# Sums of squares spread over the places of the first stage, a later first attention group, and four buffers of cosines and sines

## The chip, the cores and the metric

The kernel runs on one core of one Trainium2 chip. The metric is the device time of one execution in microseconds (us), as the median of several runs; a profiled execution gives the trace. The engines are named as in the profile: PE (TensorE, matmuls), PEld (its weight loads), DVE (VectorE), ACT (ScalarE), POOL (GpSimd) and SP (SyncE, which only issues DMAs here).

## The reference

One inference step of a hybrid encoder layer, on 2048 prompt frames and 64 frames of a running stream, 2112 tokens of width 1024 in all, in float32:

```
xn = rmsnorm(x, norm_mix)                      # x * rsqrt(mean(x*x) + eps) * g
proj = xn @ w_in                               # 1024 x 5632: x_rnn, y_gate, q, k, v, g_rnn, g_attn
xc = causal_dwconv(x_rnn); h = rg_lru(xc)      # width-4 conv, gated linear recurrence
y_rnn = h * gelu(y_gate)
q, k = rope_partial(q), rope_partial(k)        # first 16 dims of each head of 64
y_attn = band_attention(q, k, v, sinks)        # 16 heads, 4 KV heads, chunks of 64, window 128
mixed = sigmoid(g_rnn) * y_rnn + sigmoid(g_attn) * y_attn
x = x + mixed @ w_out
x = x + ConvFFN(rmsnorm(x, norm_ffn))          # up 5632, width-3 conv, silu(gate) * val, down
y = rmsnorm(x, norm_final)
```

The outputs are y and the new key, value, recurrence and convolution states.

## The kernel before

Tokens stand in the free dimension and features in the 128 partitions. A float32 matmul is done as three matmuls of rounded parts: each operand is split into a high part (a copy that rounds, on ACT, line 204) and a low part (the rest, on DVE, line 205), and `mm3` (lines 237 to 239) multiplies high by high, low by high and high by low. A tile of 128 output features of one block of tokens takes 8 k-tiles, so 24 matmuls.

The first stage, which the change touches, runs in three sets of two blocks: 320, 320, then 384, 384, then 352, 352 tokens (`SETS`). For each set the 44 column tiles of `w_in` pass by. `kept` brings a tile's weights: in the first set the raw weights are loaded (line 226, tiles `wraw`, which lie in a region of SBUF called FW), split into `whl` (three buffers), and the split form is stored to DRAM (`wiS`, on POOL's queue); in the later sets the split form is loaded from there (line 223). PSUM has three banks (`pmm`, name "mm") for the results of projections.

A set begins with q, k and v. Two tiles hold the rotated parts of q: `trig` loads a block's cosines and sines (tiles named "h", lines 395 and 396), `rope` (lines 375 to 381) multiplies the two PSUM results by them, and `qparts` splits and stores the result to DRAM (`qS`, line 390). The same follows for k, then v and the other q tiles.

Then come four groups `g`, one for each KV head. `key_prep` reads the keys and values back and splits them (kA, kB, vv). `rnn` is a generator that computes two channel tiles of the recurrent branch: 18 steps, here called places, numbered j = 0 to 17. A channel's places are two of x (with the convolution), two of y, one of the gates (lines 652 to 656) with the scan after it, two of g and two of a; most hold one projection of 24 matmuls. `attention` is a second generator, advanced once at each place: a unit of 128 queries has its scores S and softmax at one place (lines 547 to 565), its transposes (line 572) three places later, and its products Y (lines 580, 581) a place after that; in between the next unit's queries are loaded from `qS` (line 539: D twice, E once). The products of a group with the gates (`mix`) are put off to the next group's place 3.

The next set's tokens are prepared in groups 2 and 3. `stats` loads x (line 255, tiles `xk`), squares each k-tile on ACT (lines 257 and 259) and adds the squares on POOL (line 260), 16 k-tiles in a set; its `finish` makes the reciprocal root (lines 263 to 266), called at place 6 of group 3. Then `apply` scales and splits the tokens. In the kernel before, all of `stats` is written at place 8 of group 2.

What sets the order: in the first stage a scheduler that works with its own estimates of durations sorts each engine's instructions, so an instruction can stand some places ahead of where it is written; each engine then runs its list strictly in order, and SP and POOL also issue their DMAs in order. `with behind()` puts the DMAs of its block behind the last weight load on their queue. The second stage (output projection and feed-forward part) is scheduled by hand and is not touched.

Of the kernel before, what the change touches and what calls it, by code (L numbers as in the profile page):

```python
# [7 lines left out]
F32 = mybir.dt.float32  # L8
F32R = mybir.dt.float32r
AF = mybir.ActivationFunctionType  # L10
ALU = mybir.AluOpType
# [3 lines left out]
P = 128  # L15
T = 2112
TP = 2048
KO = 8
# [3 lines left out]
SETS = [[(0, 320), (320, 320)], [(640, 384), (1024, 384)], [(1408, 352), (1760, 352)]]  # L22
BN = 384
# [103 lines left out]
def kernel(ctx: ExitStack, tc: tile.TileContext, xT, w_in, w_out, w_up, w_dn, gw, pk,  # L127
                             sinks, cq, sq, ck, sk, kcT, vcT, kcn, vcn, augk, auge, ident_in,
                             yT, kpT, ksT, vpT, vsT, kc_o, vc_o, h_o, lc_o, fc_o):
    nc = tc.nc  # L130
# [21 lines left out]
    FW = Region(tc, "FW", 23712, F32)  # L152
    fw = Pool(FW)
# [61 lines left out]
    def behind():  # L215
        return tc.issue_after(lastw[0].ins)
# [30 lines left out]
        xblocks[t0] = (pool.tile([P, KO, BN], F32R, name="xh", bufs=2), pool.tile([P, KO, BN], F32R, name="xl", bufs=2))  # L247
        return xblocks[t0]

    def stats(t0, n):  # L250
        r = fw.tile([P, BN], F32, name="nr", bufs=2)[:, :n]
        s = fw.tile([P, BN], F32, name="ns", bufs=2)[:, :n]
        for k in range(KO):
            x = fw.tile([P, BN], F32, name="xk", bufs=4)[:, :n]
            nc.sync.dma_start(x, xT[k * P:(k + 1) * P, t0:t0 + n])
            if k == 0:
                nc.scalar.activation(s, x, AF.Square)
            else:
                nc.scalar.activation(x, x, AF.Square)
                nc.gpsimd.tensor_tensor(s, s, x, op=ALU.add)  # L260

        def finish():
            p = pmm.tile([P, 512], F32, name="mm")
            nc.tensor.matmul(p[:, :n], ones, s, start=True, stop=True)
            nc.scalar.activation(r, p[:, :n], AF.Sqrt, scale=1.0 / 1024, bias=epst)
            nc.vector.reciprocal(r, r)
            rstd[t0] = r
        return finish

    def apply(blocks):  # L270

# [38 lines left out]
    with tc.tile_pool(name="sp", bufs=1) as sp:  # L310
# [9 lines left out]
        for i, (t0, n) in enumerate(SETS[0]):  # L320
# [9 lines left out]
            r = sp.tile([P, BN], F32, name="nr", bufs=2)[:, :n]  # L330
# [3 lines left out]
            for k in range(KO):  # L334
                x = xt[:, k, :n]
# [3 lines left out]
        consts()  # L339

    es1 = ExitStack()

    FX = Region(tc, "FX", 4096, F32, "right")
    es1.callback(FX.close)
    fw.regions = (FW, FX)
    fw.extend("wraw", KO * P, 1)
    ap = es1.enter_context(tc.tile_pool(name="ap", bufs=1, reuse_waits="tile", side="right"))
    rp_ = es1.enter_context(tc.tile_pool(name="rp", bufs=2, reuse_waits="tile", side="right"))
    pat = es1.enter_context(tc.tile_pool(name="pat", bufs=1, space=PSUM))
# [40 lines left out]
            nc.sync.dma_start(qS[i, r0:r0 + 128, tt], t[:, :n].bitcast(F32))  # L390

    def trig(c, s, r, tt, n):
        ct = rp_.tile([P, BN], F32, name="h")
        st = rp_.tile([P, BN], F32, name="h")
        nc.sync.dma_start(ct[:r, :n], c[:, tt])
        nc.sync.dma_start(st[:r, :n], s[:, tt])
        return ct, st
# [53 lines left out]
    for si, blocks in enumerate(SETS):  # L451
# [5 lines left out]
        for t0, n in blocks:  # L457
            tt = slice(t0, t0 + n)
            ct, st = trig(cq, sq, P, tt, n)
            a, b = rope(proj(wa, t0, n), proj(wb, t0, n), P, ct, st, n)  # L460
            qparts(a[:, :n], 0, tt, n)
            qparts(b[:, :n], 128, tt, n)
# [3 lines left out]
        for t0, n in blocks:  # L466
            tt = slice(t0, t0 + n)
            ct, st = trig(ck, sk, 32, tt, n)
# [121 lines left out]
        def attention(g, kv):  # L590
            units = [attn_s(g, u, kv) for u in qts]
            next(units[0])
            for i, u in enumerate(units):
                next(u)
                if i:
                    next(units[i - 1])
                yield
                if i:
                    next(units[i - 1])
                yield  # L600
                if i + 1 < len(units):
                    next(units[i + 1])
                yield
            next(units[-1])
            yield
            next(units[-1])
            yield
# [116 lines left out]
        def rnn(g, rr, ta):  # L724
            for i in range(2):
                c, st = 2 * g + i, {}
                yield from rnn_x(c, st)
                yield from rnn_y(c, st)
                for bi in range(len(blocks)):
                    rnn_gates(c, st, bi)  # L730
                yield
                rnn_scan(c, st)
                yield from rnn_g(c, st, rr[i])
                yield from rnn_a(c, ta[i])

        nxt = []
        for g in range(4):
            kv = key_prep(g)
            ya = ap.tile([P, 2, SN], F32, name="ya")
            rr = [rp_.tile([P, SN], F32, name=f"rr{i}", bufs=1) for i in range(2)]  # L740
            ta = [[], []]
            at = attention(g, kv)
            for j, _ in enumerate(rnn(g, rr, ta)):
                next(at, None)
                if j == 3:
                    while pending:
                        pending.pop(0)()
                if g == 2 and j == 8 and si + 1 < len(SETS):
                    with behind():
                        nxt = [stats(t0, n) for t0, n in SETS[si + 1]]  # L750
                if g == 3 and j == 6:
                    for f in nxt:
                        f()
                if g == 3 and nxt:

                    if j == (16 if si == 0 else 8):
                        ahead = apply(SETS[si + 1])
                    if j in ((16, 17) if si == 0 else (9, 13, 15)):
                        with behind():
                            next(ahead)  # L760
            if g == 3 and nxt:
                for _ in ahead:
                    pass
            if g == 1 and si == 2:

                fw.close()
                xk, raws = Pool(FW), Pool(FW, right=True)
                xk.reserve("xk", BS, 16)
                raws.reserve("wraw", 4 * P, 2)
                mixed = mixes(0, xk)  # L770
                with behind():
                    next(mixed)
                    wload(0)
                    wload(1)
            if g == 3 and si == 2:

                es0.close()
                RA = Region(tc, "RA", 58368, F32R)
                mixp, wh0 = [Pool(RA), None, None], Pool(RA)
                wh0.reserve("wh", 8 * P, 4)  # L780
            for _ in at:
                if g == 3 and si == 2:
                    next(mixed)
                    next(mixed)
                    next(mixed)
            for i in range(2):
                pending.append(lambda i=i, rr=rr, ta=ta, ya=ya, g=g, blocks=blocks, s0=s0:
                               mix(2 * g + i, rr[i], ta[i], ya[:, i], blocks, s0))
# [539 lines left out]
    dmade, dloaded, dweights, draws_, toks, fetched, raw = [0] * 7, [0] * 7, {}, {}, {}, [0], {}  # L1328
# [67 lines left out]
    for i in range(3):  # L1396
# [7 lines left out]
        if i == 0:  # L1404
            xk = Pool(FW)
# [5 lines left out]
        for m in range(8):  # L1411
# [17 lines left out]
            if i == 0 and m == 5:  # L1429
                drive(side, 99)  # L1430
                xk.close()
                xk = Pool(FW, right=True)
# [49 lines left out]
    for i, (lanes, fresh, u) in enumerate(plan):  # L1482
# [61 lines left out]
        if i in (11, 18):  # L1544
            t0, n = PAIRS[2][i == 18]
# [117 lines left out]
    for j, (i, p, k, ms, cs) in enumerate(seq):  # L1663
# [54 lines left out]
        for m in ms:  # L1718
            r = {q: R[p, q][:, m, cs] for q in ("11", "12", "21", "22")}
# [152 lines left out]
```

## Time and profile before

| what | value |
| --- | --- |
| median of 3 runs | 2969.44 us (2962.66 to 2976.83) |
| profiled execution: its own time | 2964.2 us |
| profiled execution: span of the trace | 2962.4 us |
| mean granted PE clock | 0.983 |
| busy: PE, DVE, ACT, POOL | 96%, 69%, 51%, 14% |

The span runs from the first to the last instruction on the core. In rows of the timeline the first number is the start in us, the second the duration; brackets give how long the engine had been idle before and what released it. "SPq" is SP's queue of DMA issues; its duration there is that of issuing, not of the transfer. In rows of waits the numbers are the total in us, how often, and the longest. In windows the numbers behind the window's length are the busy us of PE, PEld, DVE, ACT and POOL with their instruction counts, then the PE clock granted, the DMA engines' share and GB/s.

### The profile page before, as it was taken

To read this page: it belongs to the slowest core of one execution; us is meant where nothing else is said; L and a number is where in the kernel's file an instruction comes from. 1 tells how busy PE (TensorE), PEld (TensorE's weight loads), DVE (VectorE), ACT (ScalarE), POOL (GpSimd) and SP (SyncE) were. 2 spreads that over 40 slices of the span, in tenths; PEclk is the share of its full clock that TensorE was granted. 3 is DMA by queue.
4 is the path that set the end of the run, shared out by engine and by line. 5 is a ranking of instruction groups with operands and counts; after the bars stand their busy time and mean duration, and the time that the engine had idled before them with its cause. 6 is when DMAs were issued, how large, how long until landed. Compare 5 with 4: busy or idle time off the path is not lost.

```text
span 2962.4 us, 48650 instructions
## 1 busy us (share of the span) xinstructions
PE 2856.2 (96%) x17572; PEld 2749.1 (93%) x17572; DVE 2037.4 (69%) x3998; ACT 1507.7 (51%) x3353; POOL 400.6 (14%) x699
## 2 busy tenths in 40 slices
PE   7999899999999999998898999999899999999998
PEld 6899899999999999998898999999799999999997
DVE  6388784467686277776567988888756557656686
ACT  4377772466654266665324555555544444333442
POOL 2012100000200000002321323333111111000011
PEclk8999999999999999999999999999999999999999
DMA  7867656644455745436875656565766666977573
GB/s 250 282 210 229 193 198 226 193 149 135 152 162 169 244 141 182 147 125 247 274 234 178 219 195 220 200 221 201 259 202 219 215 223 210 278 208 223 162 231 112
DMA packets 337042, 601.13 MB, mean 203 GB/s; under 512 B 39216, under 2 KB 236832, under 8 KB 319904
## 3 DMA queue, kind: packets, MB, share of 16 engines
q1 hardware_dynamic: 288096, 409.28, 44.9%
q0 software_dynamic: 48704, 188.73, 16.8%
q8 instruction: 139, 2.28, 0.3%
q14 instruction: 103, 0.84, 0.1%
HBM read 398.11 MB, written 200.29 MB: 202 GB/s over the span
## 4 chain that ended last, share of the span: by engine, by line
PE 61%; issue 15%; DVE 10%; DMA 8%; ACT 3%; POOL 2%; SPq 0%; POOLq 0%; DVEq 0%; ACTq 0%
PE mm L237 9%; PE mm L239 9%; PE mm L238 9%; PE mf L1157 3%; PE mf L1159 3%; PE mf L1158 3%; PE mf L1678 2%; PE mf L1677 2%; PE mf L1679 2%; DMA x1S<-FW 2%; PE mm L1159 2%; PE mm L1157 2%; PE mm L1158 2%; PE pt L572 2%; DMA FW<-in_xT_dram 1%
## 5 line engine op out<-in xcount | busy, mean ns | idle before, releaser
L237 PE MATMUL mm<-xh,whl 128*128 128x320 f32 (+2 forms) x2112 | 691.1, 327 | 12.6 <-DVE y L379 9.6
L238 PE MATMUL mm<-xl,whl 128*128 128x320 f32 (+2 forms) x2112 | 687.2, 325 | 5.4 <-DVE xl L205 4.7
L239 PE MATMUL mm<-xh,whl 128*128 128x320 f32 (+2 forms) x2112 | 685.9, 325 | 0.0
L209 ACT ACTIVATE RE<-FW 128x512 fp32r<-128x512 f32 (+2 forms) x540 | 288.0, 559 | 398.9 <-DVE FW L1036 98.2
L210 DVE TENSOR_TENSOR RE<-FW,RE 128x512 fp32r<-128x512 f32 (+2 forms) x540 | 313.4, 602 | 161.1 <-ACT RE L209 156.1
L237 PEld LDWEIGHTS mm<-xh,whl 128*128 128x128 f32 x2112 | 401.7, 190 | 19.7 <-DVE y L379 11.1
L238 PEld LDWEIGHTS mm<-xl,whl 128*128 128x128 f32 x2112 | 401.8, 190 | 12.2 <-DVE xl L205 8.0
L239 PEld LDWEIGHTS mm<-xh,whl 128*128 128x128 f32 x2112 | 401.4, 190 | 0.8
L1193 DVE SCALAR_TENSOR_TENSOR FA<-FA,pkt 128x608 f32<-128x608 f32 (+1 forms) x264 | 245.4, 950 | 51.1 <-ACT FA L1187 46.5
L1157 PE MATMUL mf<-RA,RE 128*128 128x304 f32 (+1 forms) x604 | 198.9, 329 | 12.5 <-ACT FW L1202 5.5
L1159 PE MATMUL mf<-RA,RE 128*128 128x304 f32 (+1 forms) x604 | 198.1, 328 | 0.0
L1158 PE MATMUL mf<-RA,RE 128*128 128x304 f32 (+1 forms) x604 | 197.5, 327 | 0.0
L1677 PE MATMUL mf<-RE 128*128 128x304 f32 (+1 forms) x594 | 192.9, 325 | 1.8 <-DVE RR L1722 1.8
L1678 PE MATMUL mf<-RE 128*128 128x304 f32 (+1 forms) x594 | 192.7, 324 | 0.6 <-DVE RE L210 0.5
L1679 PE MATMUL mf<-RE 128*128 128x304 f32 (+1 forms) x594 | 191.2, 322 | 0.0
L1158 PE MATMUL mf<-RE 128*128 128x304 f32 (+1 forms) x484 | 158.3, 327 | 4.1 <-DVE RE L210 4.1
L550 DVE TENSOR_REDUCE mx<-S 128x4 f32<-128x1024 f32 (+1 forms) x68 | 81.0, 1191 | 117.9 <-PE S L548 117.9
L1157 PE MATMUL mf<-RE 128*128 128x304 f32 (+1 forms) x484 | 158.3, 327 | 3.1 <-ACT RE L209 3.1
L1187 ACT ACTIVATE FA<-FA,pkt 128x608 f32<-128x608 f32 (+1 forms) x132 | 128.1, 970 | 64.0 <-DVE FA L1208 59.5
L1159 PE MATMUL mf<-RE 128*128 128x304 f32 (+1 forms) x484 | 158.2, 327 | 0.0
L559 ACT ACTIVATE pr<-S,nm 128x256 f32<-128x256 f32 (+1 forms) x272 | 124.0, 467 | 27.9 <-DVE nm L553 27.3
L1157 PEld LDWEIGHTS mf<-RA,RE 128*128 128x128 f32 x604 | 114.8, 190 | 17.8 <-ACT FW L1202 6.1
(335 smaller groups left out, 6954.7 us busy)
## 6 DMA issues: line engine op xcount, KB each, us to landing
whl<-wiS SPq DMA_DIRECT2D x88, 1024.0 KB, 5.3
wiS<-whl POOLq DMA_DIRECT2D x44, 1024.0 KB, 6.9
wuS<-RE POOLq DMA_DIRECT2D x88, 512.0 KB, 4.0
RE<-wuS SPq DMA_DIRECT2D x88, 512.0 KB, 4.4
FW<-in_w_up_dram SPq DMA_DIRECT2D x154, 256.0 KB, 4.1
hS<-FA POOLq DMA_DIRECT2D x154, 152.0 KB, 3.8
FW<-hS SPq DMA_DIRECT2D x154, 152.0 KB, 3.8
FW<-in_w_in_dram SPq DMA_DIRECT2D x44, 512.0 KB, 5.3
```

The costliest lines, as they stand in the source:

```text
L209: lastact[0] = nc.scalar.activation(hi, src, AF.Copy)
L210: return lambda: nc.vector.tensor_tensor(lo, src, hi.bitcast(F32), op=ALU.subtract)
L237: nc.tensor.matmul(ps[:, :n], wh[:, c], xh[:, k, :n], start=first, stop=False)
L238: nc.tensor.matmul(ps[:, :n], wh[:, c], xl[:, k, :n], start=False, stop=False)
L239: nc.tensor.matmul(ps[:, :n], wl[:, c], xh[:, k, :n], start=False, stop=last)
L1157: nc.tensor.matmul(ps[:, :n], w[:, 0, c], x[:, k, 0], start=first, stop=False, **more)
L1158: nc.tensor.matmul(ps[:, :n], w[:, 0, c], x[:, k, 1], start=False, stop=False, **more)
L1159: nc.tensor.matmul(ps[:, :n], w[:, 1, c], x[:, k, 0], start=False, stop=last, **more)
L1193: nc.vector.scalar_tensor_tensor(uc, G[:, j:j + self.cols], col("fw", 44 * j + m), uc, op0=ALU.mult, op1=ALU.add)
L1677: nc.tensor.matmul(ps[m][:, cs], w[:, 0, c], t[:, 0], start=k == 0, stop=False)
L1678: nc.tensor.matmul(ps[m][:, cs], w[:, 0, c], t[:, 1], start=False, stop=False)
L1679: nc.tensor.matmul(ps[m][:, cs], w[:, 1, c], t[:, 0], start=False, stop=k == 10)
```

## The change

It has four parts. `stats` becomes a generator over both blocks of a set: the first step loads two k-tiles, and each further step squares one k-tile, adds it and loads the one two ahead; it is advanced once at each place from place 4 of group 2 to place 4 of group 3. In the very first group the attention is not advanced at places 0 and 1, and twice at places 7 and 13. The tiles "h" get four buffers instead of two. The region FX (4096 bytes in each partition), through which the raw weights had a third buffer, goes: two raw weight buffers are left in the first set. For `apply`, the `xk` tiles have nine buffers in both kernels.

```
-    def stats(t0, n):
-        r = fw.tile([P, BN], F32, name="nr", bufs=2)[:, :n]
-        s = fw.tile([P, BN], F32, name="ns", bufs=2)[:, :n]
-        for k in range(KO):
-            x = fw.tile([P, BN], F32, name="xk", bufs=4)[:, :n]
-            nc.sync.dma_start(x, xT[k * P:(k + 1) * P, t0:t0 + n])
-            if k == 0:
-                nc.scalar.activation(s, x, AF.Square)
-            else:
-                nc.scalar.activation(x, x, AF.Square)
-                nc.gpsimd.tensor_tensor(s, s, x, op=ALU.add)
-        def finish():
...
+    def stats(blocks, done):
+        todo = [(t0, n, k) for t0, n in blocks for k in range(KO)]
+        raw = []
+        def load(j):
+            if j < len(todo):
+                t0, n, k = todo[j]
+                raw.append(fw.tile([P, BN], F32, name="xk", bufs=4)[:, :n])
+                nc.sync.dma_start(raw[j], xT[k * P:(k + 1) * P, t0:t0 + n])
+        def finish(t0, n, r, s):
...
+        load(0)
+        load(1)
+        yield
+        for j, (t0, n, k) in enumerate(todo):
+            x = raw[j]
+            if k == 0:
+                r = fw.tile([P, BN], F32, name="nr", bufs=2)[:, :n]
+                s = fw.tile([P, BN], F32, name="ns", bufs=2)[:, :n]
+                nc.scalar.activation(s, x, AF.Square)
+                done.append(lambda t0=t0, n=n, r=r, s=s: finish(t0, n, r, s))
+            else:
+                nc.scalar.activation(x, x, AF.Square)
+                nc.gpsimd.tensor_tensor(s, s, x, op=ALU.add)
+            load(j + 2)
+            yield
...
-    FX = Region(tc, "FX", 4096, F32, "right")
-    es1.callback(FX.close)
-    fw.regions = (FW, FX)
-    fw.extend("wraw", KO * P, 1)
...
-        ct = rp_.tile([P, BN], F32, name="h")
-        st = rp_.tile([P, BN], F32, name="h")
+        ct = rp_.tile([P, BN], F32, name="h", bufs=4)
+        st = rp_.tile([P, BN], F32, name="h", bufs=4)
...
             for j, _ in enumerate(rnn(g, rr, ta)):
-                next(at, None)
+                if (si, g) != (0, 0) or j > 1:
+                    next(at, None)
+                if (si, g) == (0, 0) and j in (7, 13):
+                    next(at, None)
...
-                if g == 2 and j == 8 and si + 1 < len(SETS):
+                if g == 2 and j == 4 and si + 1 < len(SETS):
+                    squares_ = stats(SETS[si + 1], nxt)
+                if si + 1 < len(SETS) and (g == 2 and j > 3 or g == 3 and j < 5):
                     with behind():
-                        nxt = [stats(t0, n) for t0, n in SETS[si + 1]]
+                        next(squares_, None)
```

Line numbers in the order of the changed kernel are higher by 9 to 15 behind `stats` (rope's stores are line 399, the loads of cosines and sines 404 and 405).

SP's queue at the start of set 1, in the kernel before (`h` are cosines and sines, `whl` weights, `qS` the stores of q):

```order
L223 DMA whl<-wiS 128x2048
L390 DMA qS<-xch 128x384
L390 DMA qS<-xcl 128x384
L395 DMA h<-in_cq_dram 128x384
L396 DMA h<-in_sq_dram 128x384
L223 DMA whl<-wiS 128x2048
L395 DMA h<-in_ck_dram 32x384
```

The same place in the changed kernel:

```order
L223 DMA whl<-wiS 128x2048
L399 DMA qS<-xch 128x384
L399 DMA qS<-xcl 128x384
L404 DMA h<-in_ck_dram 32x384
L405 DMA h<-in_sk_dram 32x384
L404 DMA h<-in_ck_dram 32x384
```

The second block's pair for q, 128x384, has gone from here; it now stands with the first block's pair in set 0, behind the first stores of k. The second weight load of the rows before now follows the second block's stores.

ACT at the beginning of the first group's places, before (`xc`, `xr`, `xch` belong to the x places, `pr` and `es` to the softmax of the first unit, `y` to the y places):

```order
L623 ACTIVATE xc<-mm,pkt 128x320
L628 ACTIVATE xr<-mm 128x320
L204 ACTIVATE xch<-xc 128x320
L559 ACT_TABLE_LOAD
L559 ACTIVATE pr,sm<-S,nm 128x128 x4
L561 ACTIVATE es<-es 128x4
L623 ACTIVATE xc<-mm,pkt 128x320
L628 ACTIVATE xr<-mm 128x320
L204 ACTIVATE whl<-FW 128x1024
L688 ACTIVATE y<-mm 128x320
```

The same in the changed kernel:

```order
L632 ACTIVATE xc<-mm,pkt 128x320
L637 ACTIVATE xr<-mm 128x320
L204 ACTIVATE whl<-FW 128x1024
L697 ACTIVATE y<-mm 128x320
L204 ACTIVATE xch<-xc 128x320
L679 ACT_TABLE_LOAD
L679 ACTIVATE y<-y 128x320
L568 ACT_TABLE_LOAD
L568 ACTIVATE pr,sm<-S,nm 128x128 x4
L570 ACTIVATE es<-es 128x4
L697 ACTIVATE y<-mm 128x320
```

The first softmax has moved behind both x places and the first y, and has a table load before it. On PE the first unit's scores stand 48 matmuls later than before.

ACT in group 2 of set 0, before, around the first y place (`FW` and `FX` in lines 257 and 259 are the squares):

```order
L204 ACTIVATE xch<-xc 128x320
L559 ACTIVATE pr,sm<-S,nm 128x128 x4
L561 ACTIVATE es<-es 128x4
L259 ACTIVATE FX<-FX 128x384
L623 ACTIVATE xc<-mm,pkt 128x320
L628 ACTIVATE xr<-mm 128x320
L204 ACTIVATE whl<-FW 128x1024
L259 ACTIVATE FW<-FW 128x384 x2
L688 ACTIVATE y<-mm 128x320
```

The same in the changed kernel (line 279 is the square):

```order
L204 ACTIVATE xch<-xc 128x320
L568 ACTIVATE pr,sm<-S,nm 128x128 x4
L570 ACTIVATE es<-es 128x4
L632 ACTIVATE xc<-mm,pkt 128x320
L637 ACTIVATE xr<-mm 128x320
L204 ACTIVATE whl<-FW 128x1024
L279 ACTIVATE FW<-FW 128x384 x2
L697 ACTIVATE y<-mm 128x320
```

Before, these two squares are the 13th and 14th of the 16 and two more follow before the second y; in the changed kernel they are the 7th and 8th, and the next pair stands at the next scan.

More of the change, by code (lines that the diff above doesn't have):

```diff
@@ L267, in finish @@
             rstd[t0] = r
-        return finish
+        load(0)
[13 more added lines that the diff above has]
+            yield
     def apply(blocks):
```

## The prediction

> **What bounds the kernel now.** I read the page, then TensorE's waits over the whole run, then the busy time and granted clock in short windows around the longest waits.
>
> ```profile
> span 2962.4 us, 48650 instructions
> ...
> PE 2856.2 (96%) x17572; PEld 2749.1 (93%) x17572; DVE 2037.4 (69%) x3998; ACT 1507.7 (51%) x3353; POOL 400.6 (14%) x699
> ```
>
> TensorE (PE) is busy 96% of the span, and its work stays as it is. Time can only come from places where PE stands still or runs at a lowered clock. Its waits (in total, times, longest):
>
> ```profile
> PE mm L237 <- DVE y L379: 9.6, 5, 3.6
> PE mm L652 <- ACT y L688: 5.8, 2, 3.6
> PE S L547 <- DMA D<-qS: 5.2, 1, 5.2
> PE Y L581 <- DVE pl L205: 4.5, 6, 2.3
> PE mm L237 <- ACT ta L475: 1.2, 1, 1.2
> ```
>
> The first row is the rope (cosines and sines), the second and fourth lie where the squares run, the third is the first group's attention. Windows show what each place costs; the reader is to take PE's first number and the clock (PEclk, then DMA share and GB/s):
>
> ```profile
> 110.00:120.00 10.00, 10.00 (x70) 10.00 (x69) 4.33 (x6) 3.21 (x5) 1.07 (x2) 1.00 0.76 258
> 120.00:130.00 10.00, 7.00 (x49) 6.48 (x47) 4.30 (x8) 3.26 (x7) 0.53 (x1) 1.00 0.98 392
> 130.00:140.00 10.00, 7.57 (x29) 7.20 (x30) 1.36 (x5) 2.94 (x10) 0.00 (x0) 0.51 0.78 214
> ...
> 300.00:310.00 10.00, 3.19 (x11) 2.13 (x11) 6.84 (x11) 7.28 (x15) 4.71 (x5) 0.71 0.90 304
> 310.00:320.00 10.00, 10.00 (x55) 9.80 (x55) 5.96 (x16) 7.20 (x17) 1.13 (x2) 0.78 0.47 158
> ...
> 750.00:760.00 10.00, 8.10 (x51) 7.25 (x50) 6.70 (x15) 9.95 (x25) 4.45 (x5) 1.00 0.84 252
> ...
> 770.00:780.00 10.00, 6.97 (x27) 6.09 (x26) 8.94 (x20) 3.49 (x12) 2.00 (x3) 0.76 0.24 57
> 780.00:790.00 10.00, 10.00 (x59) 10.00 (x59) 2.10 (x5) 2.81 (x6) 0.00 (x0) 0.90 0.36 119
> ...
> 465.00:470.00 5.00, 2.94 (x17) 2.62 (x16) 0.76 (x2) 0.00 (x0) 0.00 (x0) 1.00 1.02 397
> 470.00:475.00 5.00, 4.18 (x15) 4.18 (x16) 3.74 (x8) 1.05 (x2) 0.00 (x0) 0.66 0.47 160
> ...
> 940.00:945.00 5.00, 2.94 (x19) 2.65 (x18) 3.31 (x7) 0.53 (x2) 0.00 (x0) 1.00 0.83 291
> ```
>
> The first row is an undisturbed window, 70 matmuls in 10 us. I count as lost a window's length less PE's busy time times the clock. First attention, 120 to 140: 3.00 + (10 - 7.57 x 0.51) = 9.1 us. Squares in set 0, 300 to 320: 7.74 + 2.20 = 9.9 us. Squares in set 1, 750 to 790: 1.90 + 4.70 + 1.00 = 7.6 us. Rope: 2.06 + 2.24 in set 1, 2.06 in set 2, 1.2 in set 0 (the last wait row) = 7.6 us. Together 34.2 us: the most that the change can return at these places.
>
> **The lowered clock.** It makes 10.9 us of the 34.2 (3.7, 3.1, 2.7 and 1.4: busy time times the missing clock). The Trainium skill (TensorE: Matmul & The Clock Gate, What's actually happening) says that the array falls to half rate after an idle window of about 3.4 us and needs about 3.4 us of work to come back. By that, four stalls would cost an estimated 1.7 us each, 6.8 us, and the sum would be 30.1. The trace agrees on half rate (0.51 after 5.2 us), but the clock also fell to 0.76 after a longest wait of 2.3 us; I keep the windows.
>
> **Part 1, four buffers of cosines and sines.** Two buffers hold one block's pair, so the second block's loads wait until the first block's rope has read its own.
>
> ```profile
> 462.49 0.87 SPq L395 DMA_DIRECT2D h<-in_cq_dram  x1
> ...
> 469.24 0.56 DVE L375 TENSOR_TENSOR y<-mm,h 128x384 f32<-128x384 f32 x1 [7.15 <-DMA h<-in_cq_dram]
> ```
>
> VectorE idles 7.15 us for the load, and PE runs out of PSUM banks, which only the rope frees. With four buffers this pair is issued in the set before (the order shows it), so the wait goes: +7.6 us. The loads are the same in number; on SP they now stand ahead of a few stores of the first set, and one weight load of set 1 moves behind the second block's stores. That I cost at nothing: its tile is used two tiles later, 96 matmuls or 16 us (59 take 10 us in the window from 780), against a landing of some 5 us (row in part 4). If that cover is gone, 2 us a set.
>
> **Part 2, the first group's attention two places later.**
>
> ```profile
> 126.69 0.31 PE L239 MATMUL mm<-xh,whl 128*128 128x320 f32 x1
> 132.22 0.45 PE L547 MATMUL S<-kA,D 128*128 128x128 f32 x1 [5.21 <-DMA D<-qS]
> ...
> 134.32 0.47 PE L548 MATMUL S<-kB,E 128*128 128x128 f32 x1 [0.22 <-DMA E<-qS]
> ```
>
> The first scores stand in PE's queue ahead of projections that could run. They move behind 48 more matmuls, at 10 / 70 us a matmul 7 us: PE would reach them near 126.9 + 7 = 133.9, while D landed at 132.2 and E at 134.3. So the wait goes but for about 0.4 us, and with it the low clock: +9.1 us. What replaces it: the attention makes up its two places at places 7 and 13, where two steps stand together, and ScalarE gets two table loads more (107 to 109 in the order).
>
> ```profile
> 196.00:270.00 74.00, 57.16 (x123) 1.00 0.69 218
> ...
> 311.36 1.28 ACT L559 ACT_TABLE_LOAD   x1
> ```
>
> ScalarE is busy 57.16 of 74 us in the undisturbed stretch from 196 to 270, 77%. Two loads at 1.28 us fit in the rest. A doubled place could cost nothing, or as much as the wait removed (5.2 us each, 10.4). I take 2.5 us, near the low end, since that stretch has PE full under the same ScalarE load: net +6.6.
>
> **Part 3, the squares a k-tile per place.** In set 0:
>
> ```profile
> SPq L255 <- POOL FW L260: 12.6, 8, 3.8
> ...
> 283.61 6.32 SPq L255 DMA_DIRECT2D FW<-in_xT_dram  x3
> ...
> 303.21 0.52 ACT L259 ACTIVATE FW<-FW 128x384 f32<-128x384 f32 x1 [1.81 <-DMA FW<-in_xT_dram]
> 303.64 0.42 ACT L688 ACTIVATE y<-mm 128x320 f32<-128x320 f32 x1
> ...
> 304.11 0.57 PE L652 MATMUL mm<-xch,gh 128*128 128x320 f32 x1 [3.59 <-ACT y L688]
> ...
> L259 ACT ACTIVATE FW<-FW x22: 481/500/527, 272.7 to 766.3; 128x352 f32<-128x352 f32 x12, 128x384 f32<-128x384 f32 x10
> ```
>
> SP's loads wait 12.6 us for buffers that GpSimd's adds must free (three of them take 6.3 us); the square waits 1.81 us for its load, the eviction y L688 stands behind it, and the gates' matmuls on PE wait for y. In set 1 the burst of 0.5 us squares delays the scan instead, and the adds run beside it (part 5). The number stays 16 squares, 14 adds and 16 loads a set. Now two loads follow each weight load, two tiles ahead, and at most two squares stand together. So 8 us of ScalarE a set no longer come in one piece. What is late next: two squares still stand ahead of that y, and their loads stand behind the attention's. Between 0 and 7.7 us of wait may stay; I take 2 us in set 0 (one more 1.81 us wait) and 1 us in set 1, where fewer stand together: +7.9 and +6.6.
>
> **Part 4, two raw weight buffers instead of three in set 0** (their room goes to the cosines).
>
> ```profile
> FW<-in_w_in_dram SPq DMA_DIRECT2D x44, 512.0 KB, 5.3
> ...
> 112.52 1.05 ACT L204 ACTIVATE whl<-FW 128x1024 fp32r<-128x1024 f32 x1
> ...
> 123.31 1.05 ACT L204 ACTIVATE whl<-FW 128x1024 fp32r<-128x1024 f32 x1
> ```
>
> A load can now be issued when the split two tiles back is done. These two starts are the nearest pair, 10.8 us; less some 2.3 us for the split's two halves, 8.5 us remain against 5.3. Hidden, 0 us; if each were late by the 1.81 us above, 39 loads would cost 71 us.
>
> Sum: 7.6 + 6.6 + 7.9 + 6.6 = 28.7 us. The profiled run took 2964.2 us, so 2935.5 on its footing; the median of the three runs is 5.2 us above it, so 2969.4 - 28.7 = 2940.7, in round numbers 2940. A change under 0.5% (15 us) can hardly be told from none here: the three runs differ by 14 us.
>
> **The rivals.** First, the squares' loads stay late: DMA is busy 0.90 in the window from 300, and more weight loads now have squares' loads behind them. Then 17.5 us stay lost, 34.2 - 17.5 - 2.5 = 14.2, 2955 us. Against it: the first pair is issued about one weight load sooner. Second, the catch-up stalls: both doubled places cost a 5.2 us wait, 10.4 instead of 2.5; 20.8 us are left of the gain, 2949 us. Against it stands ScalarE at 77%.
>
> **Part 5, the third rival: VectorE and GpSimd.**
>
> ```profile
> 763.47 1.54 POOL L260 TENSOR_TENSOR FW<-FW,FX 128x352 f32<-128x352 f32 x1
> ...
> 766.88 1.58 DVE L672 TENSOR_TENSOR ti<-ti,t 128x768 f32<-128x768 f32 x1
> ...
> 818.98 0.95 DVE L672 TENSOR_TENSOR ti<-ti,t 128x768 f32<-128x768 f32 x1
> ```
>
> Beside an add of GpSimd the same VectorE operation took 1.58 instead of 0.95 us. Spread out, 28 adds can each meet a chain that PE waits for; at 0.63 to 1 us each that is 18 to 28 us given back, 2958 to 2968 us, no change. Against it: as many adds met VectorE before, and in one piece. The Trainium skill (SBUF — State Buffer, SBUF: two separate sides) calls this an exclusive lock held for the whole instruction, against VectorE's operations with two SBUF inputs; the pair of rows agrees.
>
> The fourth ends slower: weights come late with two raw buffers. It decides from 28.7 / 39 = 0.74 us a load on PE's path; at 1.2 us it costs 47 us, 2987 us. For it speaks the busy DMA (0.98 from 120), against it 3.2 us of slack at the nearest pair.
>
> **Chances and range.** Forecast 0.64, late loads 0.12, catch-up 0.14, GpSimd 0.06, weights 0.04. The forecast reaches from 2926 (all 34.2 us returned on the profiled run's footing, 2930, less 4 us of scatter between runs) to 2950; with the second rival and most of the first the range is 2926 to 2956. Faster by over 0.5% (below 2954.6): 0.64, 0.12 of the second and 0.05 of the first, 0.81; within: 0.15; slower: 0.04.
>
> **What would show it.** Right: no wait of S for D above 1 us; no VectorE wait for h at the starts of sets 1 and 2; clock 1.00 near 130, 300 and 765; L688 on ScalarE not behind a waiting square. Wrong: PE waits for S, pt or Y at the doubled places of the first group; ScalarE's squares still waiting for x by several us; the split L204 of weights waiting for its load in set 0.

## The result, and the profile after

The changed kernel takes 2940.3 us (median of 4 runs, 2938.4 to 2950.4), the kernel before, run beside it, 2967.5 us (4 runs, 2962.7 to 2976.8): a ratio of 0.9922, 95% interval 0.99 to 0.9944. A later set of runs gave 2943.6 against 2963.8 us, 0.9927 (0.99 to 0.9954). The profiled run took 2941.6 us.

The head of the page after, the span and the engines:

```profile
span 2939.9 us, 48667 instructions
...
PE 2852.1 (97%) x17572; PEld 2740.9 (93%) x17572; DVE 2036.4 (69%) x3998; ACT 1509.9 (51%) x3355; POOL 400.3 (14%) x699
```

PE's matmuls are the same in number and its busy time is 4 us less, while the span is 22.5 us less: what went is standing still and slow clock. PE's waits after (line, releaser: total, times, longest):

```profile
PE mm L237 <- DVE y L388: 4.7, 3, 3.7
...
PE Y L590 <- DVE pl L205: 2.3, 5, 1.3
...
PE mm L661 <- ACT y L697: 2.1, 2, 1.8
PE mm L661 <- ACT tr L664: 1.9, 2, 1.5
...
PE mm L237 <- ACT ta L494: 1.7, 1, 1.7
...
PE S L557 <- DMA E<-qS: 0.3, 1, 0.3
```

The rope's row was 9.6 us and is 4.7, with its longest, 3.7 us at the start of set 0, untouched. The wait of S for D (5.2) is gone, and 0.3 us of waiting for E came in its place. The wait for y was 5.8 and is 2.1. The windows that answer to those of before:

```profile
120.00:130.00 10.00, 10.00 (x71) 9.74 (x70) 4.55 (x10) 3.56 (x7) 0.53 (x1) 1.00 0.96 382
130.00:140.00 10.00, 9.61 (x66) 9.17 (x65) 5.58 (x16) 8.17 (x20) 0.53 (x1) 1.00 0.89 270
...
290.00:300.00 10.00, 6.39 (x29) 5.50 (x28) 4.49 (x8) 9.52 (x21) 3.21 (x4) 0.83 0.98 317
300.00:310.00 10.00, 10.00 (x74) 10.00 (x73) 9.12 (x17) 9.17 (x18) 2.52 (x4) 1.00 0.57 185
310.00:320.00 10.00, 8.67 (x57) 8.16 (x56) 9.90 (x19) 7.15 (x19) 4.89 (x5) 1.00 0.54 194
...
465.00:470.00 5.00, 5.00 (x31) 5.00 (x30) 2.25 (x5) 0.25 (x1) 0.00 (x0) 1.00 0.73 263
470.00:475.00 5.00, 5.00 (x31) 5.00 (x30) 0.24 (x1) 1.11 (x3) 0.00 (x0) 1.00 0.71 263
...
760.00:770.00 10.00, 10.00 (x64) 9.71 (x63) 7.87 (x20) 6.99 (x19) 1.90 (x2) 1.00 0.52 170
770.00:780.00 10.00, 10.00 (x65) 10.00 (x64) 6.17 (x16) 6.82 (x13) 2.43 (x3) 1.00 0.53 193
```

The first attention (but for 0.4 us), set 1's start and set 1's squares are full and at full clock. One place is not: from 290 to 320 us, in set 0's squares, 10 - 6.39 x 0.83 = 4.7 and 1.3 us are still lost.

**A ruler inside the trace.** The kernels shift against each other, so equal windows no longer hold equal work. The gated branch evicts y on ScalarE 48 times, 16 in each set (line 688 before, 697 after), always after the same projections. The time of the n-th y shows how far a kernel is ahead at the same work. The 8th, 16th, 17th, 32nd and 33rd of the kernel before, from ScalarE's timeline:

```profile
260.13 0.44 ACT L688 ACTIVATE y<-mm 128x320 f32<-128x320 f32 x1 [0.94 <-PE mm L239]
...
423.69 0.44 ACT L688 ACTIVATE y<-mm 128x320 f32<-128x320 f32 x1 [0.93 <-PE mm L239]
...
566.00 0.49 ACT L688 ACTIVATE y<-mm 128x384 f32<-128x384 f32 x1
...
893.22 0.49 ACT L688 ACTIVATE y<-mm 128x384 f32<-128x384 f32 x1 [0.45 <-PE mm L239]
...
1029.54 0.47 ACT L688 ACTIVATE y<-mm 128x352 f32<-128x352 f32 x1 [2.37 <-PE mm L239]
```

The same five of the changed kernel:

```profile
251.66 0.44 ACT L697 ACTIVATE y<-mm 128x320 f32<-128x320 f32 x1 [0.94 <-PE mm L239]
...
411.04 0.44 ACT L697 ACTIVATE y<-mm 128x320 f32<-128x320 f32 x1 [0.93 <-PE mm L239]
...
548.52 0.49 ACT L697 ACTIVATE y<-mm 128x384 f32<-128x384 f32 x1
...
867.44 0.49 ACT L697 ACTIVATE y<-mm 128x384 f32<-128x384 f32 x1 [0.44 <-PE mm L239]
...
1001.36 0.46 ACT L697 ACTIVATE y<-mm 128x352 f32<-128x352 f32 x1 [2.37 <-PE mm L239]
```

The differences give five stretches: set 0's start (first attention, and rope), set 0's second half (its squares), set 1's start (rope), the rest of set 1 (its squares), and set 2's start (rope). The table has the gain in each, us against the kernel before (minus is faster), for all the kernels of the next section as well, read from the same rows of their traces; the last column is the 48th y, the end of the first stage.

| kernel | set 0 start | set 0 squares | set 1 start | set 1 squares | set 2 start | first stage |
|---|---|---|---|---|---|---|
| length before | 260.1 | 163.6 | 142.3 | 327.2 | 136.3 | |
| changed | -8.5 | -4.2 | -4.8 | -8.3 | -2.4 | -28.4 |
| changed, second profile | -3.8 | -4.0 | -4.1 | -8.4 | -1.0 | -21.6 |
| rope buffers alone | -2.6 | +1.5 | -3.8 | -3.1 | -2.4 | -10.4 |
| two raw buffers alone | +1.7 | +0.2 | -0.5 | -0.4 | +0.6 | +1.7 |
| later attention alone | -5.5 | -1.8 | +0.3 | -2.0 | +0.2 | -8.8 |
| spread squares alone | -1.4 | -4.6 | +1.1 | -8.6 | -0.2 | -13.6 |
| rope and attention | -6.9 | +1.1 | -3.1 | -1.8 | -1.9 | -12.8 |
| changed, loads three ahead | -8.0 | -3.3 | -4.9 | -6.2 | -1.9 | -24.4 |
| changed, no adds | -6.7 | -6.2 | -5.0 | -8.9 | -2.4 | -29.3 |
| changed, two places skipped | -5.7 | -5.9 | -4.6 | -8.5 | -1.9 | -26.6 |
| changed, third raw buffer | -1.4 | -3.0 | -4.3 | -8.4 | -2.4 | -19.4 |
| both of these | -4.1 | -3.3 | -4.5 | -8.5 | -1.9 | -22.6 |

Two profiles of the changed kernel differ by 4.7 us in the first column and by at most 1.4 in any other. Set 0's start is therefore good to some 5 us in one profile, the other columns to 1 or 2.

### The profile page after: what moved, and what is told of

Read it like the earlier page. It is cut to its first block, busy times and chain, and to the rows that moved or that the text cites. A ratio compares the mean times of both kernels' runs of the same rounds, so it can differ in the third digit from the quotient of the medians.

```text
span 2939.9 us, 48667 instructions
## 1 busy us (share of the span) xinstructions
PE 2852.1 (97%) x17572; PEld 2740.9 (93%) x17572; DVE 2036.4 (69%) x3998; ACT 1509.9 (51%) x3355; POOL 400.3 (14%) x699
## 4 chain that ended last, share of the span: by engine, by line
PE 59%; issue 16%; DVE 11%; DMA 8%; ACT 4%; POOL 2%; SPq 0%; POOLq 0%; DVEq 0%; ACTq 0%
PE mm L237 9%; PE mm L239 9%; PE mm L238 9%; PE mf L1172 3%; PE mf L1174 3%; PE mf L1173 3%; PE mf L1693 2%; PE mf L1694 2%; PE mf L1692 2%; PE mm L1174 2%; PE mm L1172 2%; PE mm L1173 2%; PE pt L581 1%; POOL hS L1247 1%; PE mm L1693 1%
## 5 line engine op out<-in xcount | busy, mean ns | idle before, releaser
L1172 PE MATMUL mf<-RA,RE 128*128 128x304 f32 (+1 forms) x604 | 199.1, 330 | 12.8 <-ACT FW L1217 5.6
```

The lines of the kernel that those rows point to most:

```text
L1172: nc.tensor.matmul(ps[:, :n], w[:, 0, c], x[:, k, 0], start=first, stop=False, **more)
```

## The experiments

**One part at a time.** The kernel before with the four buffers (these need the room of the third raw weight buffer):

```diff
-    FX = Region(tc, "FX", 4096, F32, "right")
-    es1.callback(FX.close)
-    fw.regions = (FW, FX)
-    fw.extend("wraw", KO * P, 1)
...
-        ct = rp_.tile([P, BN], F32, name="h")
-        st = rp_.tile([P, BN], F32, name="h")
+        ct = rp_.tile([P, BN], F32, name="h", bufs=4)
+        st = rp_.tile([P, BN], F32, name="h", bufs=4)
```

> Part 1 alone, with the room it needs: four buffers of cosines and sines, two raw weight buffers; squares and attention as before. Read at the first matmul of the output projection, which started at 1360.5 us before and 1332.1 after. Theory (the parts stand for themselves): 7 to 8 us earlier, 1353, total near 2960. Rival (two raw buffers make the first set's weights late): the first set ends later than before, and less than 4 us are left, 1357 or more.

Measured: 2960.4 us (10 runs), ratio 0.9986 (0.9969 to 1.0003). The output projection began (first matmul into mf, here and below) at 1350.2 us against 1360.5. The two starts at which the rope's wait stood gained 3.8 and 2.4 us, 6.2 of the 6.4 expected there. That the whole gain is 10.3 us and not 7 to 8 is no merit of the part: 3.1 us came in set 1's squares, which it does not touch (last section). The total by itself cannot be told from no change.

The first four lines of that diff alone, so that only the third raw buffer goes:

> The kernel before with two raw weight buffers instead of three in the first set, nothing else. Theory: hidden, the output projection starts at 1360.5 us within 1.5, total as before. Rival: each of 39 loads late by 0.74 us or more on the path of TensorE, 29 us or more, 2996 us in total.

Measured: 2964.6 us, ratio 1.0001 (0.9985 to 1.0017); output projection at 1362.2 us, 1.7 later, 0.2 outside the bound expected. All of it lies in set 0's start, where one kernel differs from itself by 4.7. Two raw buffers cost nothing that can be seen, and the rival's 2996 us is out.

The later first attention alone:

```diff
             for j, _ in enumerate(rnn(g, rr, ta)):
-                next(at, None)
+                if (si, g) != (0, 0) or j > 1:
+                    next(at, None)
+                if (si, g) == (0, 0) and j in (7, 13):
+                    next(at, None)
```

> Part 2 alone: the first group's attention two places later and caught up at places 7 and 13. Theory: the 9.1 us around 130 go but for some 1 to 2.5 us of catching up; the output projection starts near 1353 us, total near 2960. Rival (the doubled places stall TensorE): waits for S, transposes or Y in the first group of over 5 us, start at 1358 us or later.

Measured: 2954.9 us, ratio 0.9972 (0.9953 to 0.999); output projection at 1351.7, near the theory's 1353. Set 0's start, where this part works, gave 5.5 of the 8.8 us; the rest came in the two stretches with the squares.

The spread squares alone: the new generator and its calls (both in the diff above), with two cosine buffers, three raw buffers and the first attention where it was.

> Part 3 alone: the squares a k-tile per place, with three raw weight buffers, two buffers of cosines and sines and the attention as before. Theory: in set 0 a wait for the squares' loads stays before the first y of group 2 (some 6 of 9.9 us lost), in set 1 nearly all of 7.6 us goes; the output projection starts near 1350 us, total near 2957. Rival (third buffer of raw weights lets loads stand earlier in the queue, so the squares' loads come in time): 1346 us or earlier.

Measured: 2959.2 us, ratio 0.9977 (0.9961 to 0.9994); output projection at 1346.9 us, between theory (1350) and rival (1346). Set 1 gained 8.6 us, set 0 only 4.6.

**Do the parts add up?** The ends of the first stage for the three parts sum to 10.3 + 8.8 + 13.6 = 32.7 us against 28.4 together. Rope and attention together, with the squares where they were:

> The kernel before with two parts of the change: four buffers of cosines and sines (with two raw weight buffers) and the later first attention; the squares stay where they were. By themselves these two ended the first stage at 1350.2 (-10.3) and 1351.7 (-8.8). Theory: they do not meet, so 1360.5 - 19.1 = 1341.4 us, and the 4.3 us by which the three single gains (32.7) exceed the whole (28.4) lie between the squares and the other two: the squares are then worth 9.3 us on top of these two, where they were worth 13.6 alone. Rival: both take time from the same start of set 0, so 1345.7 us, and the squares are worth 13.6 on top.

Measured: 2953.4 us (10 runs), ratio 0.9961 (0.9945 to 0.9976); output projection at 1347.8 us, 12.7 earlier. That is later than both expectations (1341.4 and 1345.7). By columns it is not one overlap: set 0's start gave 6.9 of the 8.1 of the two alone, and in set 0's second half, where attention alone gained 1.8, the pair lost 1.1, as the rope buffers alone lost 1.5 there. On top of this pair, the spread squares are worth 5.2 us in set 0's second half (164.6 us there against 159.4) and 6.5 in set 1's.

**The changed kernel once more.**

> The changed kernel as it stands, once more. In its first profile the FFN-up stage, whose code is the same, took 929.9 us, and 923.2 in the profile before; the kernel with the squares alone showed 928.8, the three without that part 922.8 to 925.2. If that is from one execution to the next, this profile, or those of the other kernels here with the spread squares, shows about 923 to 925 and a span near 2934; if it comes with the spread squares, all of these show 928 to 930 and the kernel without them (rope and attention) 923 to 925. First stage: 1332.1 +- 1.5 us in either case.

Measured: 2943.6 us (5 runs); the profile's span is 2951.0 us, 11 more than the first one's. The first stage ended 6.9 us later, not within the 1.5 expected, with 4.7 us of that in set 0's start. There ScalarE waits for the first group's keys, the V projection's evictions (ta L494) stand behind that, and PE waits for these, 1.7 us in the first profile and 2.9 here. The first profile, ScalarE's row and two windows:

```profile
81.70 0.74 ACT L529 ACTIVATE kB<-kr 64x640 fp32r<-64x640 f32 x1 [9.03 <-DMA kr<-kS]
...
80.00:85.00 5.00, 3.33 (x23) 3.07 (x22) 1.14 (x2) 2.95 (x5) 0.00 (x0) 1.00 0.73 246
85.00:90.00 5.00, 5.00 (x37) 5.00 (x35) 1.83 (x4) 2.33 (x4) 0.53 (x1) 1.00 0.93 269
```

The second:

```profile
83.78 0.74 ACT L529 ACTIVATE kB<-kr 64x640 fp32r<-64x640 f32 x1 [10.24 <-DMA kr<-kS]
...
80.00:85.00 5.00, 2.63 (x18) 2.36 (x17) 0.00 (x0) 1.22 (x2) 0.00 (x0) 0.96 0.84 282
85.00:90.00 5.00, 4.49 (x17) 4.49 (x18) 2.05 (x2) 2.05 (x5) 0.53 (x1) 0.50 0.58 169
90.00:95.00 5.00, 5.00 (x31) 5.00 (x31) 2.21 (x3) 2.12 (x4) 0.08 (x1) 0.86 0.97 373
```

The keys came later, PE's wait is 1.2 us longer, and it took the clock with it (0.50, then 0.86): 5 - 4.49 x 0.50 = 2.8 and 0.7 us are lost in the last two windows, against nothing in the first profile.

The FFN-up stage, whose code is the same in all kernels, took 929.8 us here, 929.9 in the first profile and 923.2 before; in each trace it is the time from the first row's start to the second's. In the changed kernel with two places skipped (below), which has the spread squares too:

```profile
L1172 PE MATMUL mf<-RA,RE x604: 300/303/743, 1545.9 to 2445.2; 128*128 128x304 f32 x97, 128*128 128x448 f32 x54
...
L1692 PE MATMUL mf<-RE x594: 296/301/711, 2467.7 to 2920.7; 128*128 128x304 f32 x133, 128*128 128x448 f32 x65
```

That is 921.8 us, and rope with attention, which has no spread squares, took 929.1. The stage has two lengths, 921 to 925 and 929 to 930 us, on both sides of the change, so the change does not set it; what does stays open. It is why the first profile gained 28.4 us in the first stage and 22.5 over the span.

**The squares that still stand in the way in set 0.** ScalarE and SP in the changed kernel:

```profile
281.37 1.21 SPq L259 DMA_DIRECT2D FW<-in_xT_dram  x2
...
285.70 1.08 ACT L204 ACTIVATE whl<-FW 128x1024 fp32r<-128x1024 f32 x1
289.27 0.94 ACT L279 ACTIVATE FW<-FW 128x384 f32<-128x384 f32 x2 [2.49 <-DMA FW<-in_xT_dram]
290.11 0.42 ACT L697 ACTIVATE y<-mm 128x320 f32<-128x320 f32 x1
```

Two squares' loads are issued at 281.4 us, a square waits 2.49 us for them, and y stands behind it. PE's waits at this place:

```profile
290.58 0.41 PE L661 MATMUL mm<-xch,gh 128*128 128x320 f32 x1 [0.35 <-ACT y L697]
...
293.05 0.42 PE L661 MATMUL mm<-xch,gh 128*128 128x320 f32 x1 [1.76 <-ACT y L697]
...
295.26 0.64 PE L661 MATMUL mm<-xch,gh 128*128 128x320 f32 x1 [1.50 <-ACT tr L664]
```

Before the change these three waits were 3.59, 2.19 and 1.04 us. The first, for the y right behind the squares, is nearly gone. The second is for the next y, which has no square directly before it: between the two y stand a split, a table load (1.28 us at 290.9) and the function on the first y.

First, the loads three ahead instead of two:

```diff
         load(0)
         load(1)
+        load(2)
         yield
...
-            load(j + 2)
+            load(j + 3)
```

> The changed kernel with the loads of the squares three ahead instead of two (the generator starts with load(0), load(1), load(2), and each place issues load(j + 3)); nothing else differs. Theory: about 6.0 us of set 0's loss stayed because a square stands ahead of y (L697) on ScalarE while its load, issued at 281.4 us behind a weight load and the attention's loads, lands only at 289.3 us. One place more is 4 to 5 us of lead, more than the 2.5 us that ScalarE waited longest for FW. So the loss between 290 and 320 us (6.0 us) falls below 2, and the output projection's first matmul comes at 1327 to 1329 us instead of 1332.1; median about 2936. Rival A: the loads are held by the four buffers (load j + 3 takes the buffer whose sum GpSimd has just used), or by the weight load ahead of them, so they land no earlier: 1331 to 1333. Rival B: the loads now push attention's q loads later on SP's queue, and those waits take the place: 1333 or later.

Measured: 2942.3 us, ratio 0.9931 (0.9911 to 0.995); output projection at 1336.1 us and set 0's second half 3.3 us ahead instead of 4.2. The theory is out. The end is rival B's by number, but it lies between those of the changed kernel's two profiles (1332.1 and 1339.0); what can be read is set 1's squares, 6.2 us ahead instead of 8.3 (set 0's, 3.3 instead of 4.2, are within the spread of one profile). With its load earlier, one more square runs ahead of this y, nine instead of eight, so that y again stands behind the pair issued last: at 283.1 us, used from 289.9 on, with the transfers 0.88 and 0.98 busy in the changed kernel's windows from 280 and 290. PE's longest wait for y stays 1.8 us.

Second, no square at the two places ahead of that y in set 0 (the pass has 19 places for 17 steps):

```diff
-                if si + 1 < len(SETS) and (g == 2 and j > 3 or g == 3 and j < 5):
+                if si + 1 < len(SETS) and (g == 2 and j > 3 and (si > 0 or j not in (9, 10)) or g == 3 and j < 5):
```

> The changed kernel, but set 0's pass takes no square at the two places j = 9 and j = 10 of the third group, so that the two squares (and their loads) that stand ahead of y (L697) on ScalarE come two places later; the two spare places of the 19 are used up. The measure is set 0's second half: from the fourth channel's second y to the eighth channel's second y, 163.6 us before, 159.5 in the changed kernel (159.4 in its second profile, 160.2 with loads three ahead, 157.4 without the adds, 164.7 with rope and attention alone). Theory: ScalarE reached y at 290.1 us after 2.5 us of waiting for a load that was still under way; without the two squares y is done about 3 us earlier, so 156 to 157.5 us, and some 3 us off the whole. Rival: the transfers between 282 and 289 us are what is late, whoever waits for them (the DMA engines are 0.94 to 0.99 busy there); then the weights or the q blocks come late instead, and it stays at 159 to 160.

Measured: 2934.9 us (6 runs), ratio 0.9912 (0.9898 to 0.9926). Set 0's second half is 157.6 us, 5.9 ahead instead of 4.2: most of the way to the theory's 156 to 157.5, and away from the rival's 159 to 160. The waits for y, and the windows:

```profile
PE mm L661 <- ACT y L697: 1.6, 2, 1.0
...
290.00:300.00 10.00, 7.53 (x41) 6.88 (x40) 6.45 (x12) 7.71 (x13) 1.08 (x2) 0.84 0.84 259
...
310.00:320.00 10.00, 9.55 (x64) 9.11 (x62) 9.90 (x20) 7.68 (x21) 3.52 (x4) 1.00 0.71 219
```

PE waits for the first y no longer, and for the second one 1.0 instead of 1.8 us. But 10 - 7.53 x 0.84 = 3.7 us still go in the first window with no square waiting right ahead of y: between the two y ScalarE waits 1.89 us for VectorE's xc and loads its table, and the gates' matmuls wait 1.5 us for tr (L664), as long as in the changed kernel. So most of what stayed here is not the squares' doing. By its median this is the fastest kernel with the whole work, but its interval overlaps that of the changed kernel: the 1.8 us show in the trace, at the limit of what one profile resolves, and not in the total.

**GpSimd's adds.** The generator without its line with the add:

```diff
                 nc.scalar.activation(x, x, AF.Square)
-                nc.gpsimd.tensor_tensor(s, s, x, op=ALU.add)
```

> The changed kernel without GpSimd's adds of the squares: the sums of squares then hold the first k-tile alone, the loads and ScalarE's squares stay. Theory: the adds lie beside work that is off the path, so the output projection starts at 1332.1 +- 1.5 us. Rival (the prediction's third): GpSimd's adds slow VectorE's operations beside them, and with them TensorE; without the adds the first stage ends at 1328 us or earlier. A third way: without the adds the load that takes a buffer over waits for ScalarE alone and not for GpSimd; then ScalarE's wait for FW gets shorter, and that gain is in the wait for y, not in VectorE's times.

Measured: 2935.0 us, ratio 0.9906 (0.9883 to 0.9929); output projection at 1331.2 us, inside the theory's bound, 0.9 us ahead of the changed kernel. Set 0's second half gained 2.0 us over it, set 1's 0.6, set 0's start (no adds there) lost 1.8. So the adds are not free, but they cost some 2.6 us by two columns that are good to 1 or 2, not 18 to 28. Where: in the changed kernel PE waits 1.33 us for VectorE at 313 us, and here that window is full.

```profile
313.30 0.50 PE L590 MATMUL Y<-pl,vv 128*128 128x512 f32 x1 [1.33 <-DVE pl L205]
```

```profile
310.00:320.00 10.00, 10.00 (x68) 9.83 (x67) 8.94 (x22) 8.34 (x22) 0.53 (x1) 1.00 0.72 225
```

What VectorE did just before, beside two adds of GpSimd in the changed kernel:

```profile
309.64 2.59 POOL L280 TENSOR_TENSOR FW<-FW 128x384 f32<-128x384 f32 x2
...
310.08 1.27 DVE L681 TENSOR_TENSOR ti<-ti,t 128x640 f32<-128x640 f32 x1
311.28 1.30 DVE L682 TENSOR_SCALAR a<-a 128x640 f32<-128x640 f32 x1
```

The same two without the adds:

```profile
311.78 0.82 DVE L680 TENSOR_TENSOR ti<-ti,t 128x640 f32<-128x640 f32 x1
312.51 0.49 DVE L681 TENSOR_SCALAR a<-a 128x640 f32<-128x640 f32 x1
```

The two operations took 0.45 and 0.81 us longer beside the adds, together about PE's 1.33 us. The expectation's third way is out: ScalarE waits as long for the squares' loads without the adds (5.2 us against 5.0 from 270 to 300), and PE's longest wait for y is 2.0 us. From 290 to 320 us the windows lose 6.0 us here too, since the clock fell further (0.76, then 0.90); the 2.0 us are read from the ruler.

**The third raw buffer back**, in the changed kernel. The cosines keep their two buffers, the sines get two in the idle part of the region FW, and FX is there again:

```diff
+    FX = Region(tc, "FX", 4096, F32, "right")
+    es1.callback(FX.close)
+    fw.regions = (FX,)
+    fw.extend("wraw", KO * P, 1)
+    fw.regions = (FW, FX)
...
-        ct = rp_.tile([P, BN], F32, name="h", bufs=4)
-        st = rp_.tile([P, BN], F32, name="h", bufs=4)
+        ct = rp_.tile([P, BN], F32, name="h")
+        st = fw.tile([P, BN], F32, name="hs", bufs=2)
```

> The changed kernel with the third raw weight buffer back (it lies in a region of its own again, and the two sine buffers lie in the idle part of the first region, so that there are still four of cosines and sines). Theory: the prediction's part 4 (a price of 0 for two raw buffers) holds, set 0's second half stays at 159.5 +- 0.7 us. Rival: two raw buffers do cost where they meet the other parts: from the ninth to the eleventh y of set 0, kernels with two raw buffers lose 1.8 to 3.1 us against the kernel before, those with three between -0.5 and +0.3; then the second half comes to 157 to 158 us.

Measured: 2949.1 us, ratio 0.9951 (0.9937 to 0.9965); set 0's second half 160.6 us. The rival's 157 to 158 is out: over the whole second half the third buffer returns nothing. The stretch that the rival named, from the ninth y to the eleventh, did come back to 39.9 us, the length before, from 41.8 in the changed kernel; but up to the ninth y 2.1 us were lost (40.6 against 38.5). The kernel is rather slower, above all in set 0's start (-1.4). The order of the instructions differs from set 0's start on, so this is not the buffer's price alone.

> Both edits together: the third raw weight buffer back, and no square at set 0's two places ahead of y. Theory: only the skipped places count, so set 0's second half is 156 to 157.5 us, as with the skip alone. Rival: both count, 153.5 to 155.5 us, and the whole is 5 us or more under the changed kernel's.

Measured: 2943.5 us, ratio 0.993 (0.9915 to 0.9945); set 0's second half 160.2 us. Neither: with three raw buffers the skip gained only 0.4 us there. Its trace shows why:

```profile
294.41 1.05 ACT L279 ACTIVATE FW<-FW 128x384 f32<-128x384 f32 x2 [3.40 <-DMA FW<-in_xT_dram]
295.42 0.53 ACT L276 ACTIVATE FW<-FW 128x384 f32<-128x384 f32 x1
295.85 0.42 ACT L703 ACTIVATE y<-mm 128x320 f32<-128x320 f32 x1
```

The scheduler still put three squares before this y, and they waited 3.40 us for their loads. So the edit did not clear the place here, and the run says nothing against the skip. The total is no better than the changed kernel's.

## Why the prediction was right, point by point

The total, 2940.0 forecast and 2940.3 measured, agrees better than the steps do, and part of that is luck: against the kernel before beside it the gain was 27.1 us in the first set of runs and 20.3 in the second, with 28.7 forecast. The mechanism of each part held; the size of one did not. Against the table:

- **Part 1, rope, 7.6 us.** Right in mechanism and size. Set 1's start gave 4.8 and 4.1 in the two profiles (4.3 forecast), set 2's 2.4 and 1.0 (2.06); alone the part gave 3.8 and 2.4. VectorE waits for no load of h any more. Of set 0's 1.2 us little is seen: the wait for ta L475 is gone, but the one for ta L494, 0.9 before, is 1.7.
- **Part 2, first attention, net 6.6 us.** The wait fell as worked out, D's whole and E at 0.3 us against the 0.4 forecast. With Part 1's 1.2 us, 7.8 were forecast for set 0's start. Two profiles of the changed kernel and four of kernels that have the same start gave 8.5, 3.8, 8.0, 6.7, 5.7 and 6.9, a mean of 6.6. Neither doubled place shows a wait of several us in these profiles; the second rival (2949 us) did not happen.
- **Part 3 in set 0, 7.9 us: the step that failed.** 4.2 us came. The prediction left 2 us of residual, "one more 1.81 us wait"; by the windows 6.0 us stayed (4.7 + 1.3), inside the 0 to 7.7 given as bounds, but its size was taken from the low end. It put the whole 9.9 us down to squares ahead of y. Taking the two squares away returned only 1.8 us (4.7 + 1.3 became 3.7 + 0.1 + 0.5). What stays in the first window is waits for the second y and for tr, and lowered clock; the 1.3 us at 313 came from VectorE slowed beside GpSimd's adds. Two of the prediction's own signs spoke against it here: y stood behind a waiting square (2.49 us), and the clock was 0.83 and not 1.00. The first rival, late loads, named the mechanism of the 1.8 us, but let it keep the whole 17.5 us of both sets, and set 1 shows none of it.
- **Part 3 in set 1, 6.6 us.** 8.3 us came, 6.5 of them on top of rope and attention, which gave 1.8 by themselves in that stretch. PE is busy for all of the changed kernel's four windows from 750 to 790.
- **Part 4, two raw buffers, 0 us.** Held: no gain in putting the third back, a ratio of 1.0001 in taking it away.
- **The third rival, GpSimd against VectorE.** The mechanism is real (1.27 against 0.82 us for the same operation and form), the price some 2.6 us. The add in the prediction's row ended at 765.0 us, before VectorE's slow operation; the one beside that was the next row of five adds (765.09 to 771.5).
- **The sum.** 7.8 + 7.9 + 4.3 + 6.6 + 2.1 forecast, 8.5 + 4.2 + 4.8 + 8.3 + 2.4 measured in the first profile, which with 0.2 after set 2's start is the 28.4 of the table. Nearly all of the 3.7 us that set 0's squares owed came from the four others, each a little above its forecast. In the second profile they did not, and the first stage gained 21.6.

## What to carry to other kernels

Measure a gain at fixed work, by the n-th occurrence of one instruction, and profile the same kernel twice before reading differences of a few us: here one stretch moved by 4.7 us between two profiles of the same kernel, and a stage whose code is the same in all kernels by 7. When a burst is spread over a schedule, look at each new place for what stands behind it on its engine. Where the transfers were full, issuing the loads one place earlier did not help; keeping their users away from the critical eviction gave 1.8 us. Before a whole window of loss is put down to one cause, each of its waits has to be followed to its own.

## What was not expected of the hardware

The clock's price of a stall was a matter of chance. At the same place in set 0's start PE waited for the V eviction in every kernel; with 2.9 us the clock fell to 0.50 (above), but without the adds, after a wait of 3.0 us:

```profile
PE mm L237 <- ACT ta L493: 3.0, 1, 3.0
...
85.00:90.00 5.00, 4.82 (x33) 4.82 (x34) 1.89 (x2) 2.14 (x5) 0.53 (x1) 1.00 0.65 182
```

it stayed at 1.00, as it did after 3.1 us with rope and attention, while 2.2 us with attention alone took it to 0.69 over 5 us. Length alone does not decide. The Trainium skill (TensorE: Matmul & The Clock Gate, What's actually happening) says that the activity window is free-running and that the point at which the clock changes depends on where in the window the first matmul lands. These rows fit that, though the waits of 2.2 and 2.9 us that lowered the clock are shorter than the idle window of about 3.4 us that the Trainium skill gives there; what decides is not shown here. The same happened in set 1's squares. The kernel before and the one with the rope buffers alone both have a longest wait of 2.3 us for Y there, but in the second the clock stayed at 1.00:

```profile
PE Y L577 <- DVE pl L205: 3.0, 2, 2.3
...
760.00:770.00 10.00, 7.68 (x46) 6.97 (x45) 9.90 (x12) 5.15 (x13) 6.00 (x5) 1.00 0.48 147
```

In the prediction's windows of set 1 the lowered clock cost 2.7 us, so it is most of the 3.1 us which that kernel gained in a stretch that it does not touch. The lowered clock was 10.9 of the 34.2 us in the prediction's windows; part of such a figure belongs to one execution and not to the kernel. By the rule of the Trainium skill (TensorE: Matmul & The Clock Gate, What's actually happening) the sum would have been an estimated 24.6 us (28.7 less 10.9 plus 6.8) instead of 28.7; two profiles of the changed kernel, at 28.4 and 21.6, do not decide between them.
